# MoBA's probabilities turned by VectorE and a trip through DRAM, branch projections by halves of two chunks, x loaded later

## The chip, the cores and the metric

The kernel runs on one core of one Trainium2 chip. The metric is device microseconds of one execution. A core has a matrix engine (TensorE, "PE" in the profile, with its weight loads shown as "PEld"), a vector engine (VectorE, "DVE"), an activation engine (ScalarE, "ACT"), GpSimd ("POOL") and SyncE ("SP"), which here only issues DMAs. Each engine works through its own instructions strictly in the order in which the program was written for it, and waits at an instruction until what it needs is there.

## What is computed

Two decoder layers on 256 tokens of 1024 features, all in float32. Each layer is a gated mixer of two attentions, then a SwiGLU. Cut to what matters here:

```python
proj = x @ w_in                       # -> q, k, v of 8 stick-breaking heads, q, k, v of 8 MoBA heads, 2 gates
o_sb = stick_breaking_attention(...)
o_mb = moba_attention(...)            # 256 tokens are one block: causal softmax(q k^T / 8) v
branch_sb = merge_heads(o_sb) @ w_branch_sb
branch_mb = merge_heads(o_mb) @ w_branch_moba
merged = sigmoid(g_sb) * branch_sb + sigmoid(g_mb) * branch_mb
x = layer_norm(alpha * x + merged @ w_out)
x = layer_norm(alpha * x + (silu(x @ w_gate) * (x @ w_up)) @ w_down)
```

## The kernel before

**Numbers in two parts.** Every float32 operand of a product is split into a rounded part ("hi", a float32r copy made by ACT) and the rest ("lo", a subtraction by DVE); a product is three matmuls, hi·hi, hi·lo and lo·hi (`mm3`, line 424). Weights come as 122 granules per layer of 128x1024 numbers (512 KB). SP loads each into one of six `raw` buffers (line 135), ACT casts it into a ring slot `whi`, and DVE subtracts into `wlo` (lines 166 and 169). The rings hold ten granules; a slot is given free (`ws.allow`) when the matmuls of its old granule have been written. Seven granules per layer go another way, by DMAs that POOL issues (lines 182 and 200).

**One order, made when the kernel is built.** A planner, `Weave`, keeps an estimated time for PE, ACT and DVE. The main program writes PE's large matmuls; everything else is a generator (a "side") that yields the estimated time at which its next step is due, and `tick` runs the due ones after each three matmuls. Whatever a step emits takes its place at that moment in each engine's order. Nothing is reordered on the chip. `finish` runs sides to their end where the program needs their result.

**Attention.** Heads are handled in four pairs p = 0 to 3. For MoBA (`mb_line`, line 663) the scores of two pairs are made together (`two_pairs`), masked, their maximum taken (DVE), exponentiated with a running sum (ACT) and scaled by the reciprocal (DVE). The probabilities are 128 queries x 768 (two heads x three blocks of 128 keys), and have to be turned, so that keys lie on the partitions. `weighted` (line 564) does that with six PE transposes into a PSUM tile `pT` and then splits it into `pp` (ACT cast, DVE subtraction), of which there is one buffer. `both_parts` (line 605) multiplies by v (four matmuls, tiles `o`), and an ACT copy and DVE adds into `f` (one buffer) and a split give `o_mb`, hi and lo.

**Turning by another way.** `bounce_line` (line 502) was there already, for q and k of MoBA and a part of the SwiGLU: DVE transposes 32x32 blocks, SP stores the tile to DRAM and loads it back in four DMAs, which put the blocks in their places.

**Gates, branches, output.** Gate chunks c = 0 to 7 (tiles `pg`, 48 matmuls each) run while the attention of the pairs is worked off. Then `weave.finish(sides)` (line 875) waits for all attention, and the branch projections follow chunk by chunk (tiles `pb`, 24 matmuls of the stick-breaking half, 24 of the MoBA half, granule `G + 40 + c` with both halves), each merged by DVE into `m` and split. The output projection (tiles `pw`) then reads `m` chunk by chunk, first for the tokens 0 to 127.

## Time and profile before

| what | value |
|---|---|
| median of three runs | 726.14 us (726.01 to 726.39) |
| the profiled execution | 726.34 us |
| its span, first to last instruction | 724.5 us |
| around the span | 1.8 us |
| instructions | 12760 |
| mean granted TensorE clock | 0.997 |
| moved by DMA | 149.96 MB, mean 207 GB/s |

A page of the profile lists each engine's busy time and groups of instructions (line, engine, operation, output<-inputs, count, busy us, mean ns, idle time of the engine before them and what ended it). The chain of waits goes back from the last instruction to whatever released it each time, and so shows what set the end. The timeline lists single instructions with start and duration; "x4" merges four, and a bracket tells how long the engine had been idle and for whom.

### The profile page before, as it was taken

The numbers are of one execution on the slowest core, as the hardware profiler recorded it, in microseconds if no ns is written. First come the engines' busy times: TensorE is split into PE (matmuls) and PEld (weight loads), VectorE is DVE, ScalarE is ACT, GpSimd is POOL, SyncE is SP. The second block draws the span as 40 slices with busy tenths as digits, with TensorE's granted clock in tenths as the row PEclk, the third lists the DMA queues.
The fourth block names the chain that finished last, engine by engine and source line by source line (L and its number), as shares of the span: only waits on it lengthen the run. The fifth ranks groups of instructions, "written<-read, shape, count | busy, mean of one in ns | idle before, by whom it ended". The sixth has DMA issues, their size and how long they took to land.

```text
span 724.5 us, 12760 instructions
## 1 busy us (share of the span) xinstructions
PE 714.0 (99%) x5032; PEld 657.0 (91%) x5032; DVE 524.1 (72%) x792; ACT 391.0 (54%) x589; POOL 33.5 (5%) x48
## 2 busy tenths in 40 slices
PE   9999999999999999999999999999999999999995
PEld 7889899998899999988889889999888999998885
DVE  5999877796886666643688887877889776665416
ACT  5767687663665554442365566775556555454300
POOL 0001110000000000000000111100010000000001
PEclk9999999999999999999999999999999999999998
DMA  8899884575596656476259679745748865663501
GB/s 294 337 340 265 266 204 139 204 216 190 181 338 211 202 181 199 146 295 197 76 179 349 163 193 245 201 126 191 267 144 285 290 203 182 199 202 96 224 1 59
DMA packets 53532, 149.96 MB, mean 207 GB/s; under 512 B 10080, under 2 KB 17248, under 8 KB 53472
## 3 DMA queue, kind: packets, MB, share of 16 engines
q1 hardware_dynamic: 49296, 134.21, 55.2%
q0 software_dynamic: 4032, 14.68, 9.0%
q8 instruction: 39, 0.64, 0.4%
q10 hardware_dynamic: 144, 0.26, 0.1%
q14 instruction: 21, 0.17, 0.1%
HBM read 144.93 MB, written 4.19 MB: 206 GB/s over the span
## 4 chain that ended last, share of the span: by engine, by line
PE 96%; DVE 2%; DMA 0%; ACT 0%; issue 0%; POOL 0%; POOLq 0%; DVEq 0%
PE l1pf L418 14%; PE l0pf L418 14%; PE l0pd L418 8%; PE l0pg L418 6%; PE l1pg L418 6%; PE l1pe L418 4%; PE l1pd L418 4%; PE l1pqk L418 3%; PE l0pqk L418 3%; PE l0pw L418 3%; PE l1pvq L418 3%; PE l0pft L418 3%; PE l1pw L418 3%; PE l1pft L418 3%; PE l0pb L418 3%; PE l1pb L418 3%
## 5 line engine op out<-in xcount | busy, mean ns | idle before, releaser
L53 DVE TENSOR_TENSOR wlo<-raw,whi 128x1024 fp32r<-128x1024 f32 (+1 forms) x234 | 277.8, 1203 | 73.6 <-ACT whi L48 70.0
L48 ACT CAST whi<-raw 128x1024 fp32r<-128x1024 f32 (+1 forms) x233 | 237.9, 1036 | 82.2 <-PE l0pd L418 19.6
L418 PE MATMUL l1pf<-xT_hi,wlo 128*128 128x256 f32 x288 | 79.6, 276 | 0.0
L418 PE MATMUL l1pf<-xT_hi,whi 128*128 128x256 f32 x288 | 79.6, 276 | 0.0
L418 PE MATMUL l1pf<-xT_lo,whi 128*128 128x256 f32 x288 | 79.6, 276 | 0.0
L418 PE MATMUL l0pf<-xT_hi,wlo 128*128 128x256 f32 x288 | 79.5, 276 | 0.0
L418 PE MATMUL l0pf<-xT_hi,whi 128*128 128x256 f32 x288 | 79.5, 276 | 0.0
L418 PE MATMUL l0pf<-xT_lo,whi 128*128 128x256 f32 x288 | 79.5, 276 | 0.0
L418 PEld LDWEIGHTS l1pf<-xT_hi,whi 128*128 128x128 f32 x288 | 54.1, 188 | 0.0
L418 PEld LDWEIGHTS l1pf<-xT_lo,whi 128*128 128x128 f32 x288 | 54.1, 188 | 0.0
L418 PEld LDWEIGHTS l1pf<-xT_hi,wlo 128*128 128x128 f32 x288 | 54.1, 188 | 0.0
L418 PEld LDWEIGHTS l0pf<-xT_hi,whi 128*128 128x128 f32 x288 | 54.1, 188 | 0.0
L418 PEld LDWEIGHTS l0pf<-xT_lo,whi 128*128 128x128 f32 x288 | 54.1, 188 | 0.0
L418 PEld LDWEIGHTS l0pf<-xT_hi,wlo 128*128 128x128 f32 x288 | 54.1, 188 | 0.0
L418 PE MATMUL l0pg<-xT_hi,whi 128*128 128x256 f32 x128 | 36.2, 282 | 0.8 <-DVE l0vmb L53 0.8
L418 PE MATMUL l1pg<-xT_hi,whi 128*128 128x256 f32 x128 | 36.0, 282 | 0.0
L418 PE MATMUL l0pg<-xT_hi,wlo 128*128 128x256 f32 x128 | 35.5, 277 | 0.0
L418 PE MATMUL l1pg<-xT_hi,wlo 128*128 128x256 f32 x128 | 35.5, 277 | 0.0
L418 PE MATMUL l0pg<-xT_lo,whi 128*128 128x256 f32 x128 | 35.5, 277 | 0.0
L418 PE MATMUL l1pg<-xT_lo,whi 128*128 128x256 f32 x128 | 35.4, 277 | 0.0
L418 PE MATMUL l0pd<-whi,l0h_hi 128*128 128x512 f32 x88 | 34.5, 391 | 0.0
L418 PE MATMUL l0pd<-wlo,l0h_hi 128*128 128x512 f32 x88 | 34.3, 389 | 0.0
(347 smaller groups left out, 1790.6 us busy)
## 6 DMA issues: line engine op xcount, KB each, us to landing
raw<-in_w_dram SPq DMA_DIRECT2D x226, 512.0 KB, 4.4
whi<-in_w_dram POOLq DMA_DIRECT2D x14, 512.0 KB, 5.6
wlo<-in_w_dram POOLq DMA_DIRECT2D x14, 512.0 KB, 7.1
ln<-in_ln_dram SPq DMA_DIRECT2D x8, 512.0 KB, 5.4
raw<-in_w_dram SPq DMA_DIRECT2D x7, 256.0 KB, 5.8
x<-in_x_dram SPq DMA_DIRECT2D x2, 512.0 KB, 8.6
out_dram<-x SPq DMA_DIRECT2D x3, 256.0 KB, 2.0
xT_raw<-in_xT_dram SPq DMA_DIRECT2D x4, 128.0 KB, 4.1
```

The source lines that it names most:

```text
L48: f(*args, **kw)
L53: f(*args, **kw)
L418: nc.tensor.matmul(o, a, b, start=start, stop=stop)
```

## The change

It does five things.

1. MoBA's probabilities are no longer turned by PE. `mb_line` hands them to a new `bounced`, which calls `bounce_line` with six blocks (a DVE transpose of 128x768, a store of 384 KB and four loads of 96 KB per pair) and then splits what came back into `pp`. Stick-breaking keeps `weighted`.
2. The scores of pairs 2 and 3 wait for the exponentials of pairs 0 and 1 (`turned.append` moves into `mb_line`), no longer for their turned tiles; the fixed pause `MB_GAP` goes.
3. Branches are computed by halves: `branch(i, b, ...)` makes two chunks 2i and 2i+1 of one branch b. The stick-breaking branch (tiles `pa`) comes first, beside the last MoBA pairs; the MoBA branch (tiles `pb`) takes heads 0 to 3 first (k = 0, 1), then k = 2, and the last pair (k = 3) last. A granule holds two chunks of one branch, which `moved` loads in pieces of 2 KB per partition from two granules of the old layout.
4. The last pair's product with v goes into PSUM tiles of the `M` kind (`in_M`) and takes no turn for the `C` kind.
5. The two loads of x (512 KB each) are issued at 118 instead of 60 on the planner's clock.

```diff
         queue.dma_start(self.raw[g][:, sl], self.w[ORDER[g], :, sl])
         self.dma_t += 0.73

+    def moved(self, start, dst, g, **kw):
+
+        b, i = divmod(g % NG_LAYER - 40, 4)
+        if 0 <= b < 2:
+            g += i - 4 * b
+            start(dst.rearrange("p (c n) -> p c n", c=2),
+                  self.w[g:g + 2, :, b * 512:(b + 1) * 512].rearrange("c p n -> p c n"), **kw)
+        else:
+            start(dst, self.w[ORDER.get(g, g)], **kw)
+
     def load(self, upto):

         while self.loaded < min(upto, len(self.hard)):
             g = self.hard[self.loaded]
             before = self.hard[self.loaded - NRAW] if self.loaded >= NRAW else None
             self._open(g)
-            self.nc.sync.dma_start(self.raw[g], self.w[ORDER.get(g, g)])
+            self.moved(self.nc.sync.dma_start, self.raw[g], g)
             self.dma_t = max(self.dma_t, self.ready.get(before, 0.0) + 0.5) + 1.46
             self.there[g] = self.dma_t + 1.0
             self.loaded += 1
...
         nc.sync.dma_start(ident, ident_in)
         nc.sync.dma_start(rope, rope_in)
         nc.sync.dma_start(mask, mask_in)
-        yield 60.0
+        yield 118.0
         for t in range(2):
             nc.sync.dma_start(xs[t], x_in[t * P:(t + 1) * P, :])

...
         for h, hs in enumerate(ROWS):
             left[i] = dve(e, S, nc.vector.tensor_sub, oT[1][hs, p, :], o[hs, h, :], oT[0][hs, p, :].bitcast(F32))

-    def both_parts(name, p, v, oT, e):
+    def bounced(name, p, src, there, v, oT, e):
+
+        pT, e = yield from bounce_line(name, there, there, src, 6, e)
+        begun.append(name)
+        mine = len(begun)
+        while len(summed) < mine:
+            yield
+        e = max(e, summed[-1])
+        yield e
+        parts = (blocked(pp[:, i].rearrange("p h (k c) -> p (h k) c", c=P)) for i in range(2))
+        e = yield from split_line(*parts, pT, 768, e)
+        yield from both_parts(name, p, v, oT, e, p == NPAIR - 1)
+
+    def both_parts(name, p, v, oT, e, in_M=False):

         turns = []
-        for h in range(2):
-            turns.append((yield from turn(e)))
-        os = [bankC(f"{name}_o{h}", [P, 2, S]) for h in range(2)]
+        if in_M:
+            os = [bankM(f"{name}_o{h}", [P, 2, S]) for h in range(2)]
+        else:
+            for h in range(2):
+                turns.append((yield from turn(e)))
+            os = [bankC(f"{name}_o{h}", [P, 2, S]) for h in range(2)]
         pe_after(e)
         for h, o in enumerate(os):
             vs = [x[:, p, 2 * h:2 * h + 2, :].rearrange("p r c -> p (r c)") for x in v]
...
         yield e
         for h, o in enumerate(os):
             for i in range(2):
-                e = left[turns[h]] = dve(e, S, nc.vector.tensor_add, f[ROWS[h]], o[ROWS[h], i, :], f[ROWS[h]])
+                e = dve(e, S, nc.vector.tensor_add, f[ROWS[h]], o[ROWS[h], i, :], f[ROWS[h]])
+            if not in_M:
+                left[turns[h]] = e
         yield e
         yield from split_line(oT[0][:, p, :], oT[1][:, p, :], f, S, e)

...
             e = dve(e, 2 * (b - a), nc.vector.tensor_reduce, nmax[:, :, i], s[:, :, a:b],
                     axis=AX.X, op=OP.max, negate=True)
         yield e
-        ex = work.tile([P, 2, 384], F32, tag="T", name=f"{name}_e")
+        flat = work.tile([P, 768], F32, tag="T", name=f"{name}_e")
+        ex = flat.rearrange("p (h c) -> p h c", h=2)
         for h, i, a, b in BLOCKS:
             e = act(e, b - a + 200, nc.scalar.activation, ex[:, h, a:b], s[:, h, a:b], AF.Exp,
                     bias=nmax[:, h, i:i + 1], accum_out=ssum[:, h, i:i + 1])
         done.append(name)
+        turned.append(e)
         yield e
         rec = small.tile([P, 2, 2], F32, tag="rec", name=f"{name}_rec")
         dve(e, 32, nc.vector.reciprocal, rec, ssum)
         for h, i, a, b in BLOCKS:
             e = dve(e, b - a, nc.vector.tensor_scalar, ex[:, h, a:b], ex[:, h, a:b], rec[:, h, i:i + 1],
                     None, op0=OP.mult)
-        yield from weighted(name, p, ex, v, oT, e)
+        if p < 2:
+            there = (page0 if p else work).tile([P, 768], F32, tag="T", name=f"{name}_turn")
+        else:
+            there = unit(f"{name}_turn", [P, 1024])[:, :768]
+        yield from bounced(name, p, flat, there, v, oT, e)

     def two_pairs(line, name, ps, qks, free, e, sides, *args):

...
         def mb_two(p):
             while len(sigmoids) < NPAIR:
                 yield
-            yield weave.t + MB_GAP * p
             yield from two_pairs(mb_line, f"{L}mb", (p, p + 1),
                                  [[[part[:, i, :] for part in t] for t in (q_mb, k_mb)] for i in (p, p + 1)],
                                  l * 2 * NPAIR + NPAIR + p, 0.0, sides, v_mb, o_mb, exps)

         for p in (0, 2):
             sides.append(weave.add(mb_two(p)))
+        mb = len(sides)
         for c in range(1, KC):
             gate(c, G + 24 + 2 * c)
-        weave.finish(sides)
-        for dst in waiting:
-            act(0.0, 512, nc.scalar.activation, dst, dst, AF.Sigmoid)
+
+        def rooted():
+            for dst in waiting:
+                act(0.0, 512, nc.scalar.activation, dst, dst, AF.Sigmoid)
+            waiting.clear()
+
+        def branch(i, b, ps, ks=range(4)):
+            g = G + 40 + 4 * b + i
+            hi, lo = (x.rearrange("p (c k n) -> p c k n", c=2, k=4) for x in ws.take(g))
+            o = (o_sb, o_mb)[b]
+            for c in range(2):
+                for k in ks:
+                    mm3(ps[:, c, :], hi[:, c, k, :], lo[:, c, k, :], o[0][:, k, :], o[1][:, k, :],
+                        c == k == 0, c == 1 and k == 3)
+            if ks[-1] < 3:
+                return 0.0
+            ws.allow(g + NSPLIT)
+            gated = gates[i][:, :, b, :]
+            return dve(pe_done(), 512, nc.vector.tensor_mul, gated, gated, ps)
+
+        if len(exps) == NPAIR:
+            rooted()
+        for i in range(4):
+            if i % 2 == 0:
+                ps = bankB(f"{L}pa{i}", [P, 2, 2, S])
+            branch(i, 0, ps[:, i % 2])
+        weave.finish(sides[:mb])
+        weave.finish(sides[:-2])
+        rooted()


         gb = load_gb(l, 0)
         m_t = [pair_tiles(f"{L}m{i}", [P, 4, S]) for i in range(2)]

-        def m_parts(c):
-            return m_t[c // 4][0][:, c % 4, :], m_t[c // 4][1][:, c % 4, :]
-
-        banks = {}
-        for c, b in ((0, 0), (1, 0), (0, 1), (1, 1), *((c, b) for c in range(2, KC) for b in range(2))):
-            g = G + 40 + c
-            hi, lo = ws.take(g)
-            hi = hi.rearrange("p (b k n) -> p b k n", b=2, k=4)
-            lo = lo.rearrange("p (b k n) -> p b k n", b=2, k=4)
-            if b == 0:
-                banks[c] = bankM(f"{L}pb{c}", [P, 2, S])
-            ps, o = banks[c], (o_sb, o_mb)[b]
-            for k in range(4):
-                mm3(ps[:, b, :], hi[:, b, k, :], lo[:, b, k, :],
-                    o[0][:, k, :], o[1][:, k, :], k == 0, k == 3)
-            if b == 0:
-                continue
-            ws.allow(g + NSPLIT)
-            mt = work.tile([P, 2, S], F32, tag="T", name=f"{L}mt{c}")
-            dve(pe_done(), 512, nc.vector.tensor_mul, mt, gates[c // 2][:, c % 2], ps)
-            e = dve(0.0, S, nc.vector.tensor_add, mt[:, 0, :], mt[:, 0, :], mt[:, 1, :])
-            weave.add(split_line(*m_parts(c), mt[:, 0, :], S, e), e)
+        def m_parts(c, n=1):
+            return [m[:, c % 4:c % 4 + n, :] if n > 1 else m[:, c % 4, :] for m in m_t[c // 4]]
+
+        pbs = [x for i in range(2) for x in bankB(f"{L}pb{i}", [P, 2, 2, S]).rearrange("p i c n -> i p c n")]
+        for ks, upto in ((range(2), -1), (range(2, 3), None)):
+            for i in range(3):
+                branch(i, 1, pbs[i], ks)
+            weave.finish(sides[:upto])
+        for i in range(4):
+            e = branch(i, 1, pbs[i], range(3 if i < 3 else 0, 4))
+            a, b = (gates[i][:, :, j, :] for j in range(2))
+            e = dve(e, 512, nc.vector.tensor_add, a, a, b)
+            weave.add(split_line(*m_parts(2 * i, 2), a, 512, e), e)


         norms = []
```

Where the instructions stand now, in three places of layer 0 (layer 1 has the same pattern in all three).

PE, the product of the last pair (`l0mb3_o`) with v. Before, 42 matmuls into a gate chunk (`l0pg6`) stood between pair 2's product and pair 3's, and these rows are how pair 2's product ended and the 42 began:

```order
L418 MATMUL l0mb2_o1_1543<-pp_168,l0vmb0_800 128x512
L418 MATMUL l0mb2_o1_1543<-pp_168,l0vmb1_801 128x2x128
L418 MATMUL l0pg6_1484<-xT_hi_108,whi_98 128x256
L418 MATMUL l0pg6_1484<-xT_lo_109,whi_98 128x256
L418 MATMUL l0pg6_1484<-xT_hi_108,wlo_99 128x256
```

Now 18 matmuls of the stick-breaking branch (`l0pa2`) stand between the two products. These are the last three of them, the last pair's product, and the first of the MoBA branch (`l0pb0`):

```order
L427 MATMUL l0pa2_1679<-l0osb_hi_328,whi_98 128x256
L427 MATMUL l0pa2_1679<-l0osb_lo_329,whi_98 128x256
L427 MATMUL l0pa2_1679<-l0osb_hi_328,wlo_99 128x256
L427 MATMUL l0mb3_o0_1751<-pp_168,l0vmb0_798 128x512
L427 MATMUL l0mb3_o0_1751<-pp_168,l0vmb1_799 128x2x128
L427 MATMUL l0mb3_o1_1752<-pp_168,l0vmb0_798 128x512
L427 MATMUL l0mb3_o1_1752<-pp_168,l0vmb1_799 128x2x128
L427 MATMUL l0pb0_1766<-l0omb_hi_1020,whi_98 128x256
```

So the last pair's product moved nearer to that of the pair before it, and the MoBA branch stands right behind it.

DVE, from the adds of pair 2 to the first merge (`raw47` to `raw50` are the weight granules that the subtraction into `wlo` belongs to). Before:

```order
L53 TENSOR_TENSOR l0mb2_f_1555<-l0mb2_o0_1542,l0mb2_f_1555 64x256 x2
L53 TENSOR_TENSOR l0mb2_f_1555<-l0mb2_o1_1543,l0mb2_f_1555 64x256 x2
L53 TENSOR_TENSOR pp_168<-l0mb3_pT_1522,pp_168 128x768
L53 TENSOR_TENSOR l0omb_lo_1023<-l0mb2_f_1555,l0omb_hi_1022 128x256
L53 TENSOR_TENSOR wlo_99<-raw44_1267,whi_98 128x1024
L53 TENSOR_TENSOR l0mb3_f_1620<-l0mb3_o0_1608,l0mb3_f_1620 64x256 x2
L53 TENSOR_TENSOR l0mb3_f_1620<-l0mb3_o1_1609,l0mb3_f_1620 64x256 x2
L53 TENSOR_TENSOR wlo_99<-raw45_1283,whi_98 128x1024
L53 TENSOR_TENSOR l0omb_lo_1023<-l0mb3_f_1620,l0omb_hi_1022 128x256
L53 TENSOR_TENSOR l0mt0_1707<-l0gate0_937,l0pb0_1668 128x512
```

Now, ahead of the first merge:

```order
L53 TENSOR_TENSOR l0mb2_f_1727<-l0mb2_o0_1718,l0mb2_f_1727 64x256 x2
L53 TENSOR_TENSOR l0mb2_f_1727<-l0mb2_o1_1719,l0mb2_f_1727 64x256 x2
L53 TENSOR_TENSOR pp_168<-l0mb3_turn_1415,pp_168 128x768
L53 TENSOR_TENSOR l0gate3_1455<-l0gate3_1455,l0pa2_1679 128x2x256
L53 TENSOR_TENSOR wlo_99<-raw47_1491,whi_98 128x1024
L53 TENSOR_TENSOR l0omb_lo_1021<-l0mb2_f_1727,l0omb_hi_1020 128x256
L53 TENSOR_TENSOR l0mb3_f_1777<-l0mb3_o0_1751,l0mb3_f_1777 64x256 x2
L53 TENSOR_TENSOR l0mb3_f_1777<-l0mb3_o1_1752,l0mb3_f_1777 64x256 x2
L53 TENSOR_TENSOR wlo_99<-raw48_1504,whi_98 128x1024
L53 TENSOR_TENSOR wlo_99<-raw49_1537,whi_98 128x1024
L53 TENSOR_TENSOR l0omb_lo_1021<-l0mb3_f_1777,l0omb_hi_1020 128x256
L53 TENSOR_TENSOR wlo_99<-raw50_1556,whi_98 128x1024
```

A gate product and two more weight subtractions have come in between. The merges of all eight chunks follow now in one piece, where they stood chunk by chunk between the weight subtractions before:

```order
L53 TENSOR_TENSOR l0gate0_935<-l0gate0_935,l0pb0_1766 128x2x256
L53 TENSOR_TENSOR l0gate0_935<-l0gate0_935 128x2x256
L53 TENSOR_TENSOR l0gate1_1131<-l0gate1_1131,l0pb0_1766 128x2x256
L53 TENSOR_TENSOR l0gate1_1131<-l0gate1_1131 128x2x256
L53 TENSOR_TENSOR l0gate2_1306<-l0gate2_1306,l0pb1_1767 128x2x256
L53 TENSOR_TENSOR l0gate2_1306<-l0gate2_1306 128x2x256
L53 TENSOR_TENSOR l0m0_lo_1763<-l0gate0_935,l0m0_hi_1762 128x512
L53 TENSOR_TENSOR l0gate3_1455<-l0gate3_1455,l0pb1_1767 128x2x256
L53 TENSOR_TENSOR l0gate3_1455<-l0gate3_1455 128x2x256
L53 TENSOR_TENSOR wlo_99<-raw51_1666,whi_98 128x1024
L53 TENSOR_TENSOR l0m0_lo_1763<-l0gate1_1131,l0m0_hi_1762 128x512
```

SP, the trips of pairs 2 and 3 among the weight loads (`scr` is the tile in DRAM), where before only weight loads stood:

```order
L134 DMA raw45_1442<-in_w_dram 128x2x512
L518 DMA l0mb2_scr_1379<-l0mb2_turn_1378 128x768
L134 DMA raw46_1477<-in_w_dram 128x2x512
L518 DMA l0mb3_scr_1416<-l0mb3_turn_1415 128x768
L134 DMA raw47_1491<-in_w_dram 128x2x512
L137 DMA raw48_1504<-in_w_dram 128x1024
L523 DMA l0mb2_turn_1378<-l0mb2_scr_1379 32x4x192 x4
L137 DMA raw49_1537<-in_w_dram 128x1024
L137 DMA raw50_1556<-in_w_dram 128x1024
L523 DMA l0mb3_turn_1415<-l0mb3_scr_1416 32x4x192 x4
L421 DMA x0_106<-in_x_dram 128x1024
```

Ten new DMAs and the first load of x stand among the weight loads, and each is issued only when the one ahead of it has been.

More of the change, by code (lines that the diff above doesn't have):

```diff
@@ L181, in cast_line @@
             self.parts[g] = [self._part(i, g) for i in range(2)]
-            e = weave.pool(weave.t, nc.gpsimd.dma_start, self.parts[g][0], self.w[ORDER.get(g, g)])
+            e = weave.pool(weave.t, self.moved, nc.gpsimd.dma_start, self.parts[g][0], g)
             self.dma_t = max(self.dma_t, e + 1.0) + 2.2
@@ L199, in rest_line @@
                 yield e
-            e = weave.pool(e, nc.gpsimd.dma_start, lo, self.w[ORDER.get(g, g)], accum_op=OP.add)
+            e = weave.pool(e, self.moved, nc.gpsimd.dma_start, lo, g, accum_op=OP.add)
             self.dma_t = max(self.dma_t, e + 1.0) + 2.2
@@ L251 @@
 MARGIN = 0.29
-MB_GAP = 8.85
 T0 = 4.1
```

## The prediction

> **What bounds the kernel.** I read the page's busy times and chain first, then its groups, then the chain and the timelines of the stretch that changes.
>
> ```profile
> span 724.5 us, 12760 instructions
> PE 714.0 (99%) x5032; PEld 657.0 (91%) x5032; DVE 524.1 (72%) x792; ACT 391.0 (54%) x589; POOL 33.5 (5%) x48
> PE 96%; DVE 2%; DMA 0%; ACT 0%; issue 0%; POOL 0%; POOLq 0%; DVEq 0%
> L418 PE MATMUL l0pg<-xT_hi,whi 128*128 128x256 f32 x128 | 36.2, 282 | 0.8 <-DVE l0vmb L53 0.8
> 72.00:135.00 63.00, 62.20 (x523) 59.62 (x522) 50.54 (x94) 43.93 (x89) 6.02 (x9) 1.00 0.71 203
> ```
>
> PE is at work in 714.0 of 724.5 us and makes 96% of the chain. So whatever leaves PE's queue shortens the run, and whatever makes PE wait lengthens it. The fourth row holds the one wait of PE in mid-kernel, 0.8 us. The last is the MoBA stretch of layer 0 (us, then PE, PEld, DVE, ACT and POOL busy, clock, DMA share, GB/s): PE at 62.2 of 63 us and full clock, DVE with 12.5 us to spare.
>
> **What leaves PE.** The chain through that stretch (start, us, what):
>
> ```profile
> 101.89 0.66 PE l0mb_pT L431 x6
> 102.55 1.06 PE l0pg L418 x9
> 103.61 0.66 PE l0mb_pT L431 x6
> ...
> 111.18 1.57 PE l0mb_s L550 x24
> 112.75 0.89 PE l0mb_o L418 x4
> ...
> 125.93 0.70 PE l0mb_o L418 x4
> 126.62 4.82 PE l0pg L418 x42
> 131.44 0.70 PE l0mb_o L418 x4
> 132.14 2.77 PE l0pg L418 x24
> 134.91 21.76 PE l0pb L418 x192
> 156.67 3.47 PE l0pw L418 x15
> ```
>
> The six transposes of a pair take 0.66 us, and there are eight pairs in two layers: 8 x 0.66 = 5.3. Around them matmuls start a little late: single rows at 101.61 and 102.50 enclose a pair's six and one more matmul,
>
> ```profile
> 101.61 0.28 PE L418 MATMUL l0pg<-xT_hi,wlo 128*128 128x256 f32 x1
> 101.73 0.82 PE L431 MATMUL l0mb_pT<-ident,l0mb_e 128*128 128x128 f32 x6
> 102.30 0.37 PE L418 MATMUL l0pg<-xT_hi,whi 128*128 128x256 f32 x1
> 102.50 0.28 PE L418 MATMUL l0pg<-xT_lo,whi 128*128 128x256 f32 x1
> ```
>
> 0.89 us where two matmuls would take 2 x 21.76/192 = 0.23, thus 0.66 to 0.70 a pair with the last start. A product with v right behind scores costs 0.89, not 0.70; that place is gone, some 0.1 per layer net of another switch. **Gain: 5.6 us** (5.3 to 5.9). The matmuls of the branches are the same 384, only in another order.
>
> **The wait at 79 us stays.** Loading x later takes 1 MB out of the DMA queues there, and ACT waited for k's trip just then (last row). But DVE was the one PE waited for:
>
> ```profile
> 77.39 0.96 DVE L53 TENSOR_TENSOR l0sb_beta<-l0sb_beta,l0sb_inc 128x766 f32<-128x766 f32 x1
> 78.27 0.68 DVE L53 TENSOR_TENSOR l0kmb_lo<-l0kmb_tok,l0kmb_hi 128x512 fp32r<-128x512 f32 x1
> 78.87 0.68 DVE L53 TENSOR_TENSOR l0vmb<-l0pu,l0vmb 128x512 fp32r<-128x512 f32 x1
> 78.69 0.62 ACT L48 CAST l0kmb_hi<-l0kmb_tok 128x512 fp32r<-128x512 f32 x1 [2.57 <-DMA l0kmb_tok<-l0kmb_scr]
> ```
>
> DVE goes back to back through its three rows, and none of them needs that cast; so v's subtraction, for which PE waits, could not have started sooner, and the order there is unchanged. I take 0, with -0.8 as the other end. In its new place x is covered: it is read only after the output projection, over 20 us later.
>
> **First new wait: the last pair.** `bounced` emits the subtraction into `pp` and, for the last pair, the product with v in the same step. PE has 18 matmuls (2.0 us) since pair 2's product; before it had 42 (4.82). What lies between those two products on ACT and DVE I read from pair 2 to 3 before:
>
> ```profile
> 126.31 0.76 ACT L48 COPY l0mb_f<-l0mb_o 64x256 f32<-64x256 f32 x2 [0.43 <-PE l0mb_o L418]
> 127.09 0.80 ACT L48 CAST pp<-l0mb_pT 128x768 fp32r<-128x768 f32 x1
> ...
> 127.24 1.78 DVE L53 TENSOR_TENSOR l0mb_f<-l0mb_o,l0mb_f 64x256 f32<-64x256 f32 x4
> 129.05 0.96 DVE L53 TENSOR_TENSOR pp<-l0mb_pT,pp 128x768 fp32r<-128x768 f32 x1
> ```
>
> From pair 2's product (start 125.93) to `pp` ready (130.01) are 4.1 us. Now a weight subtraction ends at about the same place ahead of the adds, and I reckon 4.0. PE arrives after 0.70 + 18 x 0.1133 = 2.74. **PE waits 1.25 us per layer, 2.5 in all.** Ends: were the adds late by another weight subtraction, 1.2 more each; were they to start with ACT's first copy, 0.4 less. Everything behind on PE waits with it.
>
> **Second new wait: the output projection.** From there DVE has a list without a gap. Its spacing, start to start, I read where rows followed one another:
>
> ```profile
> 139.10 0.69 DVE L53 TENSOR_TENSOR l0mt<-l0gate,l0pb 128x512 f32<-128x512 f32 x1 [2.80 <-PE l0pb L418]
> 139.82 0.42 DVE L53 TENSOR_TENSOR l0mt<-l0mt 128x256 f32<-128x256 f32 x1
> 140.16 1.22 DVE L53 TENSOR_TENSOR wlo<-raw,whi 128x1024 fp32r<-128x1024 f32 x1
> 141.30 0.68 DVE L53 TENSOR_TENSOR l0mt<-l0gate,l0pb 128x512 f32<-128x512 f32 x1
> ```
>
> A weight subtraction takes 1.14, 512 columns 0.60 (78.27 to 78.87 above), 0.71 if the next row needs the result, 256 columns 0.34. After `pp`: gate product 0.60, weights 1.14, `omb_lo` of pair 2 0.42, ACT's copy, which waits for it since `f` has one buffer, 0.45, four adds 1.74, two weights 2.28, `omb_lo` of pair 3 0.34, weights 1.14, three merges 3 x 1.31, and `m_lo` of the first two chunks 0.68: 12.7 us, less 0.08 overlap at the start. PE in that time: 0.70 for the product, 96 x 0.1133 = 10.88 for the MoBA branch, then 0.45 until the third matmul of `pw` (2 x 3.47/15), the first that reads `m_lo`: 12.05. **PE waits 0.6 per layer.** In layer 0 the next `m_lo` stands behind another weight subtraction, 0.3 more; in layer 1 it is ahead of it. On the way `omb_lo` of pair 3 is ready 7.0 us after `pp` by the same list, and PE asks for it after 0.70 + 55 x 0.1133 = 6.9: nothing worth a term. **1.5 us in all**, ends 0 (DVE 0.7 faster per layer) and 3.0 (whole durations in place of the spacings, 0.7 more per layer).
>
> **What is hidden.** DVE's transposes of 768 columns have no row; those of 256 and 512 have,
>
> ```profile
> L53 DVE STREAM_TRANSPOSE l0hb<-l0sg 128x256 f32<-128x256 f32 x4 | 1.8, 446 | 0.1
> L53 DVE STREAM_TRANSPOSE l0kmb_tok<-l0kmb_tok 128x512 f32<-128x512 f32 x2 | 1.4, 711 | 0.1
> l0kmb_scr<-l0kmb_tok SPq DMA_DIRECT2D x2, 256.0 KB, 3.5
> l0kmb_tok<-l0kmb_scr SPq DMA_DIRECT2D x8, 64.0 KB, 6.9
> l1kmb_scr<-l1kmb_tok SPq DMA_DIRECT2D x2, 256.0 KB, 7.0
> raw<-in_w_dram SPq DMA_DIRECT2D x226, 512.0 KB, 4.4
> 92.11 9.78 PE l0pg L418 x84
> 99.77 0.24 ACT L48 ACTIVATION_READ_ACCUMULATOR l0mb_e<-l0mb_s,l0mb_nmax 128x1 f32 x1
> ```
>
> and 0.265 more for each 256 gives 0.98, an estimate: 3.9 us per layer within the 12.5 that DVE has free; without that cover they would add to the chain above at 0.98 each. A trip through DRAM has a store (3.5 to 7.0 us to landing) and loads (4.4 to 6.9). In layer 0 the scores of pairs 2 and 3 now follow 75 matmuls after the first scores, at 92.11 + 75 x 0.1164 = 100.8 (the row at 92.11: 9.78/84) instead of 111.18; the exponentials whose PSUM they take are done at 100.0, 0.8 ahead. SP holds pair 2's store behind weight loads that wait for DVE to free a `raw` buffer: one subtraction waits, through ACT, for gate chunk 5, 138 matmuls behind the scores, near 118; so I put the store at 116, the loads, behind two more weight loads, at 124 to 125, landed by 132. Pair 2's product comes 201 + 42 + 69 matmuls and two products behind the scores, 102.4 + 312 x 0.1145 + 1.4 = 139.5, and ACT and DVE need 2.5 us ahead of it for the split: 5 us to spare. Pair 3's loads land some 3 us later and its product is due 4 us later. Behind the waiting DMAs stand weight loads for granules used more than 10 us later, so those can wait. The branch weights in 2 KB pieces I cost at nothing for the same reason: even twice 4.4 us lies inside that lead.
>
> **Sum.** Against the profiled execution, 726.34: -5.6 + 2.5 + 1.5 = -1.6. That execution lies 0.2 above the median of the three, 726.14, so I forecast **724.5**, 0.2% less, about what a measurement of this kernel can tell from no change.
>
> **Rivals.**
>
> *The merges hide* (second wait 0, the first near 0.8): for it speaks that DVE had slack in this stretch; against, that its list has no gap between `pp` and `m_lo`. -5.6 + 1.6 = -4.0: 722.1.
>
> *DVE's list is longer than its spacing says* (whole durations, or one weight subtraction more ahead of the adds): waits of 5.5 instead of 4.0, 726.0, no change to be seen.
>
> *The turned pairs come late,* the way to slower. ACT's cast of a turned pair stands ahead of weight casts, so a late load stops both. From a landing 5 us later than reckoned each further us is one on PE, in each layer; from 6.5 us the run is slower than before by what can be told. If store and loads took half as long again at their longest (7.0 + 6.9, thus 7 more), they would be late by 2 per layer: -1.6 + 4 = +2.4, 728.5. For it speaks that issues sit behind weight loads; against it that loads with the same pattern landed in 6.9 in their slowest group. The Trainium skill has a rule against this way of turning: VectorE: DVE Perf Modes, "The three transpose paths" and "Rules for kernel authors", would turn 128x128 on TensorE and warns that a plain DMA with strides is 19 times slower than the one with a transpose unit, 1309 ns for 128x128 in its table; by that I estimate 25 us for each of a pair's six blocks, which nothing here would hide. The rows of k's trip do not agree: its four loads together moved 256 KB within 6.9 us each, since DVE has turned the 32x32 blocks and the DMA moves whole runs.
>
> *The change doesn't do what it says on the path* (transposes gone, but PE waits for the same DVE work anyway, 5.6 given back): 726.1.
>
> **Chances.** Forecast 48% (723.7 to 725.4, half of it beyond 0.2% faster), merges hide 26%, longer list 13%, late 8%, given back 5%. Faster by over 0.2% (below 724.7): 0.26 + 0.27 = 0.53. Slower by over 0.2%: 0.08. Within: 0.39. Range 721.5 to 726.8: it covers the forecast, the merges' case and most of the longer list and of the given back, and leaves out the late turn and a case without any wait (720.5).
>
> **What would show it.** No transposes of MoBA on PE, 48 fewer instructions. A wait of PE of about 1.25 us for DVE's `pp` ahead of the last pair's product, in both layers, and one of 0.3 to 0.9 for `m_lo` at the start of `pw`; 0.8 still at 79 us; no wait for the turned tiles. I am wrong if PE waits for ACT's `pp` cast or for `whi` (late trips), or if it doesn't wait at all.

## The result, and the profile after

| | before | changed kernel |
|---|---|---|
| median, four runs each | 726.12 us (726.01 to 726.39) | 734.78 us (734.4 to 735.09) |
| ratio to before, 95% interval | | 1.0116 (1.0104 to 1.0129) |
| profiled execution, and its span | 726.34 and 724.5 us | 734.4 and 732.5 us |
| last matmul ends, in the span | 716.42 us | 724.85 us |

The change makes the kernel 8.7 us slower. The forecast was 1.6 us faster, and the range ended at 726.8.

The page of the changed kernel, its span, busy times and shares of the chain:

```profile
span 732.5 us, 12710 instructions
PE 712.8 (97%) x4984; PEld 652.8 (89%) x4984; DVE 529.2 (72%) x784; ACT 389.1 (53%) x579; POOL 34.5 (5%) x48
PE 92%; DVE 4%; DMA 2%; issue 1%; ACT 0%; POOL 0%; DVEq 0%; POOLq 0%; SPq 0%; ACTq 0%
```

The 48 transposes are gone (4984 matmuls for 5032), and PE is busy for 1.2 us less. But the span is 8.0 us longer, and DVE's share of the chain has doubled: PE now waits. For what, the view of waits says (engine and line that waited, for whom; us in total, times, longest):

```profile
PE l0pb L427 <- DVE l0gate L53: 2.4, 2, 1.4
PE l1pb L427 <- DVE l1gate L53: 2.4, 2, 1.4
PE l0pa L427 <- DVE l0gate L53: 1.6, 2, 0.9
PE l1pa L427 <- DVE l1gate L53: 1.6, 2, 0.8
...
PE l1mb_o L427 <- DVE pp L53: 0.8, 1, 0.8
PE l0mb_o L427 <- DVE pp L53: 0.8, 1, 0.8
```

The waits for `pp` were forecast. The four rows above them were not: in each layer PE stops twice in `pa` and twice in `pb` until DVE has multiplied a gate by a branch's product (`l0gate<-l0gate,l0pa`). The timeline of PE shows the stop, here all four in layer 0:

```profile
132.99 0.28 PE L427 MATMUL l0pa<-l0osb_hi,wlo 128*128 128x256 f32 x1
134.12 0.38 PE L427 MATMUL l0pa<-l0osb_hi,whi 128*128 128x256 f32 x1 [0.85 <-DVE l0gate L53]
134.34 0.28 PE L427 MATMUL l0pa<-l0osb_lo,whi 128*128 128x256 f32 x1
...
139.62 0.28 PE L427 MATMUL l0pa<-l0osb_hi,wlo 128*128 128x256 f32 x1
140.67 0.39 PE L427 MATMUL l0pa<-l0osb_hi,whi 128*128 128x256 f32 x1 [0.78 <-DVE l0gate L53]
...
153.03 0.28 PE L427 MATMUL l0pb<-l0omb_hi,wlo 128*128 128x256 f32 x1
154.30 0.39 PE L427 MATMUL l0pb<-l0omb_hi,whi 128*128 128x256 f32 x1 [0.99 <-DVE l0gate L53]
...
155.66 0.28 PE L427 MATMUL l0pb<-l0omb_hi,wlo 128*128 128x256 f32 x1
157.36 0.39 PE L427 MATMUL l0pb<-l0omb_hi,whi 128*128 128x256 f32 x1 [1.43 <-DVE l0gate L53]
```

Matmuls of this size otherwise start every 0.114 us. So the bracket says too little: from start to start PE loses 1.13 - 0.11, and the first matmul behind a stop takes 0.22 (134.12 to 134.34), 0.11 more than the others. That makes 1.12, 1.05, 1.27 and 1.70 us, 5.1 per layer, **10.3 in all**. DVE's side of the first stop:

```profile
133.37 0.69 DVE L53 TENSOR_TENSOR l0gate<-l0gate,l0pa 128x512 f32<-128x512 f32 x1 [3.92 <-ACT l0mb_f L48]
```

DVE was idle, began as soon as the 24 matmuls of branch half 0 were through (the last ends at 133.27; the copy that the bracket names ends at the same moment, 133.29), took 0.69, and only then did PE begin half 1. Nothing of half 1 needs that result. What ties the two together is the place where they lie: `ps = bankB(f"{L}pa{i}", [P, 2, 2, S])` is made for i = 0 and 2 only, one tile of 4 KB per partition, and halves 0 and 1 are its two parts of 2 KB; so are 2 and 3, and in `pb` likewise. In the program's order, printed with what each instruction waits for, the first matmul of half 1 carries a wait of its own:

```
L427 MATMUL l0pa0_1609<-l0osb_hi_328,wlo_99 128x256
L427 MATMUL l0pa0_1609<-l0osb_hi_328,whi_98 128x256 [waits DVE_49]
```

So the program lets the second part of a tile be written only after the last reader of its first part. Before, every chunk had a 2 KB tile (`bankM`) to itself, and was read once, when both of its halves were done.

### The profile page after: what moved, and what is told of

The parts are those of the page before. It is cut to its first block, busy times and chain, and to the rows that moved or that the text cites. A ratio compares the mean times of both kernels' runs of the same rounds, so it can differ in the third digit from the quotient of the medians.

```text
span 732.5 us, 12710 instructions
## 1 busy us (share of the span) xinstructions
PE 712.8 (97%) x4984; PEld 652.8 (89%) x4984; DVE 529.2 (72%) x784; ACT 389.1 (53%) x579; POOL 34.5 (5%) x48
## 4 chain that ended last, share of the span: by engine, by line
PE 92%; DVE 4%; DMA 2%; issue 1%; ACT 0%; POOL 0%; DVEq 0%; POOLq 0%; SPq 0%; ACTq 0%
PE l1pf L427 13%; PE l0pf L427 13%; PE l0pd L427 8%; PE l0pg L427 6%; PE l1pg L427 6%; PE l1pe L427 4%; PE l1pd L427 4%; PE l1pft L427 3%; PE l0pw L427 3%; PE l1pqk L427 3%; PE l0pft L427 3%; PE l1pvq L427 3%; PE l1pw L427 3%; PE l0pqk L427 2%; PE l0pv L427 2%; PE l1pk L427 2%
## 5 line engine op out<-in xcount | busy, mean ns | idle before, releaser
L427 PE MATMUL l0pd<-whi,l0h_lo 128*128 128x512 f32 x88 | 34.3, 389 | 0.0
```

Of the source, the lines that this page charges most:

```text
L427: nc.tensor.matmul(o, a, b, start=start, stop=stop)
```

## Experiments

**Theory A:** the tiles shared by two branch halves make PE wait, 10.3 us. **Theory B:** VectorE's list is too long in this stretch, and PE waits for it wherever that shows first. **Theory C:** the turned pairs, or the branch weights in 2 KB pieces, come late. In the table, each time stands beside that of the kernel before on the same chip.

| run | this | before | ratio, 95% |
|---|---|---|---|
| x1_pa_tiles | 731.12 | 726.46 | 1.0058 (1.0039 to 1.0078) |
| x2_own_tiles | 726.57 | 726.46 | 0.9996 (0.9984 to 1.0007) |
| b1_before_shared | 735.36 | 726.46 | 1.0109 (1.0084 to 1.0134) |
| z1_bounce_alone | 742.16 | 726.46 | 1.0200 (1.0165 to 1.0236) |
| w1_merge_order | 725.32 | 726.30 | 0.9989 (0.9980 to 0.9998) |
| y3_late_product | 727.32 | 726.30 | 1.0008 (0.9999 to 1.0018) |
| x3_x_early | 726.49 | 726.30 | 0.9999 (0.9990 to 1.0009) |
| d1_double_turn | 735.34 | 726.30 | 1.0125 (1.0110 to 1.0140) |
| w2_pw_bank | 725.48 | 726.37 | 0.9989 (0.9980 to 0.9998) |
| w5_product_later | 727.36 | 726.37 | 1.0014 (1.0005 to 1.0023) |
| w4_weights_held | 731.53 | 726.37 | 1.0066 (1.0054 to 1.0079) |
| w7_pool_adds | 731.64 | 726.46 | 1.0073 (1.0059 to 1.0087) |
| z6_half_turned | 727.94 | 726.60 | 1.0013 (1.0003 to 1.0022) |

### Tiles: x1, x2, b1

x1 only pairs the halves of `pa` in another way, so that neighbours in time lie in different tiles:

```diff
+        pas = []
         for i in range(4):
-            if i % 2 == 0:
-                ps = bankB(f"{L}pa{i}", [P, 2, 2, S])
-            branch(i, 0, ps[:, i % 2])
+            if i < 2:
+                pas.append(bankB(f"{L}pa{i}", [P, 2, 2, S]))
+            branch(i, 0, pas[i % 2][:, i // 2])
```

> The changed kernel, with one thing altered: the MoSA-side branch products (pa) alternate between the two 4 KB PSUM tiles (branches 0 and 2 in one, 1 and 3 in the other; before 0 and 1, 2 and 3). Theory A (a PSUM tile shared by two branches makes the second branch's first matmul wait until VectorE has read the first branch out): the two waits of PE inside pa, 1.12 and 1.05 us from start to start with the slow matmul behind each, go from both layers: 2 x 2.17 = 4.3 less, 730.4; the waits ahead of the last pair's product and inside pb stay. Theory B (VectorE's list is too long there and PE waits for it wherever it stands): the same time is waited ahead of pair 2's or pair 3's product, and the time stays within 1 us of 734.8. Theory C (turned pairs, or branch weights in 2 KB pieces, come late): PE waits sooner for pair 2, again 734 to 735.

x2 also gives each half of `pb` a tile of its own:

```diff
-        pbs = [x for i in range(2) for x in bankB(f"{L}pb{i}", [P, 2, 2, S]).rearrange("p i c n -> i p c n")]
+        pbs = [bankC(f"{L}pb{i}", [P, 2, S]) for i in range(2)]
+        pbs += [bankB(f"{L}pb{i}", [P, 2, 2, S])[:, 0] for i in range(2, 4)]
```

> As the run with pa's tiles altered, and the four MoBA-side products (pb) in a PSUM tile of their own each (two 2 KB tiles that the pairs' products leave, two halves of the 4 KB tiles). Theory A: the two waits inside pb, 1.27 and 1.70 us with the slow matmul behind each, go as well: 2 x (2.17 + 2.97) = 10.3 less than the changed kernel, 724.5; if the first halves of the output projection then wait for m_lo (0.6 per layer by the prediction), 725.7. Theory B: little of it is won, over 730. The wait of about 1 us per layer ahead of the last pair's product stays under both.

b1 does the reverse to the kernel before: two chunks in one tile.

```diff
             if b == 0:
-                banks[c] = bankM(f"{L}pb{c}", [P, 2, S])
+                if c % 2 == 0:
+                    two = bankB(f"{L}pb{c}", [P, 2, 2, S])
+                banks[c] = two[:, c % 2]
```

> The kernel before, with one thing altered: the eight chunks of the branch projections lie two by two in the 4 KB PSUM tiles, not each in a tile of 2 KB of its own. Nothing is turned through DRAM here and nothing is read or written twice in one bank. Theory A: four times per layer (chunks 1, 3, 5, 7) PE waits for VectorE to have read the chunk before out of the other half: 1.1 us each, where VectorE is free, 8 x 1.1 = 8.8 more, 734.9. Theories B and C: no such wait, 726.1.

(The "MoSA side" of the first of these texts is the stick-breaking branch.) x1 wins 3.7 of 4.3 us and x2 8.2 of 10.3 (4.0 and 8.55, if each run is taken against the kernel before on its own chip). In both, as in b1, every engine has the same instructions in the same order as the kernel that was edited; only the tiles differ. b1, which has nothing of the change but the sharing, is 8.9 slower, and its waits are where theory A puts them, four per layer:

```profile
PE l0pb L418 <- DVE l0mt L53: 3.6, 4, 0.9
PE l1pb L418 <- DVE l1mt L53: 3.5, 4, 0.9
```

This is shown from both sides: the sharing makes the slowdown. What x2 falls short of the 10.3 is told by its own waits, of which x1 has the first two as well:

```profile
PE l0mb_o L427 <- DVE pp L53: 1.2, 1, 1.2
PE l1mb_o L427 <- DVE pp L53: 1.2, 1, 1.2
...
PE l0pw L427 <- DVE l0m_lo L53: 0.4, 1, 0.4
```

In layer 0 pair 2's product begins 2.2 us sooner than in the changed kernel (139.29 for 141.47), but the last pair's `pp` is ready only 1.75 sooner (143.44 for 145.19). From start to start, with the slow matmul behind it, the wait for `pp` thus grows from 1.15 to 1.57 us per layer, and the wait of the output projection for `m_lo`, which was hidden behind the other stops, comes out: 0.78 in layer 0 (0.58, and 0.20 at the next `m_lo`) and 0.58 in layer 1. Those are 2.2 us given back; 10.3 - 2.2 = 8.1, and 8.2 was measured.

### The turning alone: z1, d1, z6

z1 takes the bounce into the kernel before, and with it the earlier scores of pairs 2 and 3; projections, weights and x stay as they were.

```diff
-        yield from weighted(name, p, ex, v, oT, e)
+        yield from bounced(name, p, flat, there, v, oT, e)
...
-            yield weave.t + MB_GAP * p
```

> The kernel before, with the turning of MoBA's probabilities through DRAM alone (scores of pairs 2 and 3 early, as in the change); branch projections in the old order with all four pairs done ahead of them, weights in 4 KB pieces, x loaded at the old time. Theory A: the transposes leave PE (5.6 less) and nothing is waited for on account of shared tiles: 720.5 to 722.5. Theory C (the trips through DRAM come late, or the extra transposes of VectorE put it behind): PE waits ahead of the products of pairs 2 or 3, which now stand some 10 us earlier relative to the projections' end: 726 or more.

16 us slower by the medians (its four executions lie between 739.8 and 743.8): here theory C holds. The chain through layer 0 (start, us, what), in the longest of the four:

```profile
127.87 6.68 DMA l0mb_turn<-l0mb_scr
134.56 0.02 issue
...
135.52 0.97 DVE pp L53
136.49 0.14 issue
136.62 0.99 PE l0mb_o L427 x2
...
140.53 0.97 DVE pp L53
141.50 0.14 issue
141.64 1.62 PE l0mb_o L427 x4
```

PE had come to pair 2's product at 131. Its data landed at 134.6, and pair 3 then stands behind one more round of product, copy, adds and `pp`. In the changed kernel pair 2's tile landed at 131.1 and pair 3's at 135.5, and that is early enough, since most of the stick-breaking branch (78 of 96 matmuls) lies ahead of pair 2's product, which begins at 141.5: there is no wait for a turned tile in its list of waits, nor one for `whi`. So theory C is out for the change as it stands. That the new order of the branches is what hides the trips is read from the two traces; no run took that order alone.

d1 gives the transposes of the kernel before twice, into the same place:

```diff
-                transpose(pT[:, h, cs], wt[:, h, cs])
+                for _ in range(2 if len(v[0].shape) == 4 else 1):
+                    transpose(pT[:, h, cs], wt[:, h, cs])
```

> The kernel before, with each of MoBA's 48 transposes on TensorE given twice into the same place. It measures the gain alone: the prediction's price (0.66 to 0.70 us for the six of a pair, eight pairs) makes it 5.3 to 5.6 slower, 731.4 to 731.8. Were part of a transpose hidden beside other work of PE, less; were there something behind them that waits, more.

9.0 slower, not 5.5, and the reason lies in the edit: the condition holds for the stick-breaking pairs too, so 96 transposes came twice. The chain shows a pair's twelve (start, us, what):

```profile
103.60 1.31 PE l0mb_pT L431 x12
```

Six more take 0.655; 16 x 0.655 = 10.5, and the wait at 79 us, 0.96 from start to start, is gone here because PE comes later. That leaves 9.5 for 9.0 measured. The price per pair is confirmed; that one gets it back by taking them away is not.

z6 therefore turns only pairs 0 and 1 through DRAM, in the old order of the projections, and takes the MoBA-side terms in the order of pairs 2, 3, 0, 1.

```diff
+        if p < 2:
+            yield from bounced(name, p, flat, there, v, oT, e)
+        else:
+            yield from weighted(name, p, ex, v, oT, e)
```

> The kernel before, with only pairs 0 and 1 turned through DRAM, whose trips have the time (their exponentials are done some 10 us ahead of those of pairs 2 and 3); pairs 2 and 3 are turned on TensorE as before; branch projections in the old order with the tiles of their own, the MoBA-side terms taken in the order of pairs 2, 3, 0, 1. If the gain of the prediction is real as a gain (0.66 us for the six transposes of a pair, with nothing that waits in their place), four groups less make 2.6: 723.5, and up to 1 us per layer back where the last pair's product stands right ahead of the projections: 723.5 to 725.5. Rival (on this kernel VectorE, not TensorE, sets the end of this stretch, so what leaves TensorE comes back as a wait): 726 or more.

Its list of waits for PE:

```profile
PE l1mb_o L427 <- DVE pp L53: 2.0, 1, 2.0
...
PE l0mb_o L427 <- DVE pp L53: 1.3, 1, 1.3
```

From start to start these are 2.1 and 1.5 us, together more than the 2.6 saved, and behind the longer one the granted clock fell to half for 3.41 us in the profiled execution (last section). The eleven executions lie between 726.48 and 728.7, none below the kernel before by more than that kernel's own scatter. In layer 0 the four products now stand between 118.8 and 134.4 us, where before they stood between 105.5 and 131.3, and between two products stands a chain of ACT and DVE (copy, four adds, cast, `pp`) that PE cannot shorten. So on this kernel turning less on PE was no gain even without shared tiles.

### What is left: w1, w2, y3, w5, w4, w7, x3

x2 is level with the kernel before, though PE has 5.6 us less to do. The view by stretches (us, then PE, PEld, DVE, ACT and POOL busy, clock, DMA share, GB/s) says why; first the kernel before, then x2:

```profile
137.00:157.00 20.00, 20.00 (x177) 19.92 (x176) 17.66 (x29) 12.10 (x19) 0.00 (x0) 1.00 0.70 230
```

```profile
137.00:157.00 20.00, 18.34 (x148) 17.37 (x147) 19.05 (x30) 10.88 (x18) 0.00 (x0) 1.00 0.75 247
```

DVE is busy for 19.05 of 20 us. And x2's chain of waits holds no work of PE from 139.84, ACT's copy behind pair 2's product, to 156.53, the first matmul that reads `m_lo`; three of its pieces:

```profile
139.84 0.37 ACT l0mb_f L48
142.48 0.96 DVE pp L53
155.87 0.61 DVE l0m_lo L53
```

So DVE, with ACT's share of the chain, and not PE, sets the pace here. w1 splits each merged pair of chunks as soon as the next one's sum is given:

```diff
-            weave.add(split_line(*m_parts(2 * i, 2), a, 512, e), e)
+            merges.append(weave.add(split_line(*m_parts(2 * i, 2), a, 512, e), e))
+            weave.finish(merges[:i])
```

> The run with own tiles, and the merges taken apart: the split of branch i's sum (m_lo) is put on VectorE's list right behind the sum of branch i+1, no longer behind all three. Theory A (what is left over the kernel before is the two waits of the prediction, for pp and for m_lo): m_lo of the first two chunks is ready 1.3 us sooner, so the wait at the start of the output projection, 0.58 to 0.78 us per layer there, goes: 1.4 less than the run with own tiles, 725.2. Rival (PE is held there by the weights or by something else in the list): 726.6.

725.32, as expected, and with w2 the fastest of all: 0.1% below the kernel before (0.9980 to 0.9998), too little to build on. y3 adds a `yield e + MARGIN` ahead of the last pair's product, which holds it back until its operand is due on the planner's clock, lets all four halves of `pb` do their first three quarters ahead of the last (`range(4)` and `range(3, 4)` in the loops), and has each merge's split finished ahead of the matmuls of `pw` that read it:

> The run with the merges taken apart, and the last pair's product given when its operand is due by the planner: it comes 24 branch matmuls (2.7 us) later in PE's order, and all four MoBA-side products do their first three quarters ahead of the last ones. Theory A: the wait for pp (1.41 us and 0.16 of slow matmuls per layer in the run with own tiles) goes, 3.1 less; VectorE's list from pp to the first m_lo is the next to be waited for, up to 1 us per layer back: 721.5 to 724. Rival (a wait moved is a wait kept: the same VectorE list ends at the same time whatever PE's order): 725 or more.

```profile
PE l0pw L427 <- DVE l0gate L53: 2.1, 1, 2.1
```

The wait for `pp` is gone, and one of 2.1 stands at the output projection in its place, in layer 1 as well: the rival. The row names a gate product, and there is a reason in the tiles again: `pw` takes the 4 KB tile that half 2 of `pb` leaves. w2 therefore swaps the tiles of w1 (halves 0 and 1 in `bankB`, 2 and 3 in `bankC`):

> The run with the merges taken apart, with the four MoBA-side products in their own tiles the other way round: the first two in the 4 KB tiles, the last two in the 2 KB tiles, so that the output projection's first 4 KB tile is the one that the first branch leaves, not the third. Theory A (the same rule: a tile makes its next writer wait for its last reader): the wait at the start of the output projection, 0.39 us per layer for the third branch's gate product, goes: 0.8 less than 725.3, 724.5. Rival (m_lo or the weights hold it there too): 725.3.

725.48, no gain: the wait for the gate product goes, and PE waits later in `pw` for weights (`wlo`) instead, from start to start 0.3 us in layer 0 and 0.6 in layer 1. The remaining three have the late product with it: w5 alone, w4 with the weight subtractions held back, w7 with the tiles mixed and the sums on GpSimd (`nc.gpsimd.tensor_tensor` in place of `nc.vector.tensor_add`).

> The run with the other order of tiles, and the last pair's product 24 branch matmuls (2.7 us) later in PE's order, three branches ahead of the last quarter as in the change. Theory A: the wait of 1.4 us and 0.16 of slow matmuls per layer for pp goes (3.1 in all); VectorE's list from pp to the last pair's omb_lo, three weight subtractions among it, ends near 150 and PE asks for it near 148.6, so up to 1.4 per layer comes back there: 721.5 to 724. Rival (as in the run with the late product, a wait moved is a wait kept): 724.5 or more.

> As the run with the later product, and the weight subtractions for granules three or more ahead are held back on VectorE's list from the last pair's pp until the second merge is given. Theory A (VectorE's list in that stretch is what PE waits for, and nothing else): omb_lo and the first m_lo come 1 to 2.3 us sooner, no wait is left between pp and the output projection: 726.1 - 5.6 and 0.5 for waits that are as before = 720.5 to 721.5. Rival (weights held back are late afterwards, or their raw buffers stop SP's loads): waits for whi or wlo in the output projection, 723 or more.

> The run with the later product, with the first MoBA-side product in the first 4 KB tile, the second and third in the 2 KB tiles and the fourth in the second 4 KB tile (the wait of 0.77 us per layer for the last pa gate product goes: 1.5 less than 727.4), and the four sums of two gated products per layer on GpSimd, not VectorE. Theory A (from the last pair's pp to the output projection's weights, VectorE's list is what PE waits for): three sums of 0.65 less ahead of the weight subtractions take away the 1.5 us per layer that the output projection waits for its weights: 722.5 to 724.5. Rival (GpSimd takes over 1.5 us for a sum of 128x512, and m_hi and m_lo come later by it): 725.5 or more.

All three fall to their rivals, w7 though its rival's condition (over 1.5 us for a sum on GpSimd) was not met. The longest waits of PE, one fence for each of w5, w4, w7, and the group of the sums on GpSimd:

```profile
PE l0pw L427 <- DVE wlo L53: 1.3, 1, 1.3
```

```profile
PE l0pw L431 <- DVE wlo L53: 2.7, 1, 2.7
```

```profile
PE l0pw L427 <- DVE wlo L53: 2.2, 1, 2.2
L58 POOL TENSOR_TENSOR l0gate<-l0gate 128x512 f32<-128x512 f32 x4 | 5.5, 1380 | 39.9 <-DMA raw<-in_w_dram 38.6 <-DVE l0gate L53 1.2
```

In every one of them PE ends up waiting for the weights of the output projection, whose subtractions stand on DVE behind the merges; held back in w4, they come later still. w5 and w4 also wait 0.8 us per layer at half 1 of `pb`, whose 4 KB tile the last gate product of `pa` still reads; w7, which has other tiles, waits 1.0 us per layer in `pb` for ACT's `omb_hi`. A sum takes 1.38 us on GpSimd and 0.69 on DVE, and the weight subtractions stand behind splits that wait for it. Theory B thus accounts for what remains after theory A: the edits to PE's order mostly chose which item of DVE's list was waited for. That a shorter list would win the 5.6 us is not shown, since w7, meant to shorten it, put a slower sum into the same chain.

x3 sets x2's x loads back to 60.

> The run with own tiles, and x loaded at the old time (60 on the planner's clock, not 118). The prediction costs this edit at nothing: within 0.5 of the run with own tiles, 726.6. Rival (the 1 MB in the queues matters, for the wait at 79 us or for the loads of the turned pairs): over 1 us away from it, to either side.

726.49 beside 726.57: loading x later costs and brings nothing.

## Why the prediction was wrong, point by point

**The step that failed** is a sentence of the part on what leaves PE: "The matmuls of the branches are the same 384, only in another order." Their number is right, and I looked for new waits at two places only, at `pp` and at `m_lo`. I did not ask where the sums of the halves lie and who reads the neighbouring part. That step was costed at nothing and measured 10.3 us in the changed kernel's timeline; x2 took 8.2 of it away again, and b1, by sharing alone, made the old kernel 8.9 slower. It was not among the rivals either; the only way to slower that I priced was a late trip. Nor could the signs of being wrong catch it: none of them came, and the wait for `pp` did. No run was needed to see it: the tile is in the diff, and the program's order names the wait at the instruction.

**The rest of the sum**, against rows and start-to-start distances of the profiled executions:

| term | forecast | measured |
|---|---|---|
| transposes and the late starts around them | -5.6 | -5.6 (4.6 in `pT`, 1.0 in `pg`) |
| wait for the last pair's `pp` | +2.5 | +2.3; in x2 +3.1 |
| wait of `pw` for `m_lo` | +1.5 | 0, hidden behind the stops; in x2 +1.4 |
| wait at 79 us | 0 | 0.8 still there; x3 tells no difference |
| turned pairs | hidden | no wait; z1 shows what they cost uncovered |
| weights in 2 KB pieces | hidden | weight loads to landing 4.7 us (4.4 before), no wait |
| stops at shared tiles | not seen | +10.3 |
| small waits (`omb` of pair 2, `pw`, `pft`) | 0 | about +1.4 |

The measured terms add to -5.6 + 2.3 + 10.3 + 1.4 = +8.4, and the ends of the last matmuls differ by 724.85 - 716.42 = 8.43; the medians differ by 8.7.

**What held.** The gain, both forecast waits (in x2, where nothing hides them, 1.57 per layer for 1.25 and 0.78 and 0.58 for 0.9 and 0.6), the landing of pair 2's tile in layer 0 (131.1 for 132), and the price of the transposes on DVE. That the changed kernel's own wait for `pp` (1.15) is near the forecast too is in part luck: `pp` was ready 3.7 us after pair 2's product began, not 4.0, since the stops had let DVE catch up, and a slow first matmul of 0.16 that the forecast leaves out made up for it; in x2 it was ready after 4.15. The rows for the transposes and trips:

```profile
L53 DVE STREAM_TRANSPOSE l0mb_turn<-l0mb_e 128x768 f32<-128x768 f32 x4 | 3.9, 979 | 0.1
l0mb_scr<-l0mb_turn SPq DMA_DIRECT2D x4, 384.0 KB, 4.9
l0mb_turn<-l0mb_scr SPq DMA_DIRECT2D x16, 96.0 KB, 5.3
l1mb_scr<-l1mb_turn SPq DMA_DIRECT2D x4, 384.0 KB, 8.0
```

0.979 us for 128x768 where I estimated 0.98 from the smaller rows, stores of 4.9 and 8.0 us (3.5 to 7.0 taken as bounds) and loads of 5.3. The rule of the Trainium skill against turning by DMA (VectorE: DVE Perf Modes, "The three transpose paths"), by which I estimated 25 us for each of a pair's six blocks, is about a copy that turns by its strides. It does not hold for a DMA that moves blocks which DVE has turned: these rows answer it. z1 shows that its advice can be right for another reason: where nothing covers the trip, PE waited up to 5.4 us at a pair. Two slips of mine changed nothing: 6.9 us for k's loads is a median, and single ones took up to 8.4 in layer 0; and half of 48% is 0.24, not the 0.27 in the chances.

**What was right but too small a thought:** "From there DVE has a list without a gap." I used it for one wait. x2's chain shows that it holds for the whole stretch, and the runs from w1 to w7 agree: with the tiles put right, 5.6 us less on PE came out as 1 us at the most (w1), and the forecast of -1.6 would have met +0.1 (x2).

**Open:** whether the halves need those waits on the chip, had the program not asked for them, was not tried; x2 removes the sharing, not the wait alone. And w1's 0.1% is too little to call it a better kernel.

## What to carry to other kernels

When work is reordered, list for each accumulator where it lies, who reads it, and what is written beside it in the same tile: here a tile was released whole, and a round trip PE to VectorE and back cost 1.05 to 1.70 us each time, eight times over. Then look at the program's order with its waits, not only at the order of names. And before taking work off the busiest engine, check in that very stretch how much the next engine has free; here it was 12% (17.66 of 20 us busy), and in x2 5% (19.05).

## What was not expected of the hardware

**A long wait costs more than its length.** The timeline of PE in w4, where it waited 3.1 us from start to start, and the view by stretches right behind it:

```profile
155.83 0.40 PE L431 MATMUL l0pw<-whi,l0m_hi 128*128 128x512 f32 x1
158.95 0.79 PE L431 MATMUL l0pw<-wlo,l0m_hi 128*128 128x512 f32 x1 [2.72 <-DVE wlo L53]
159.54 0.63 PE L431 MATMUL l0pw<-whi,l0m_lo 128*128 128x512 f32 x1
159.96 0.63 PE L431 MATMUL l0pw<-whi,l0m_hi 128*128 128x512 f32 x1
160.39 0.63 PE L431 MATMUL l0pw<-wlo,l0m_hi 128*128 128x512 f32 x1
```

```profile
159.00:162.50 3.50, 3.50 (x9) 2.78 (x10) 3.50 (x4) 2.30 (x4) 0.00 (x0) 0.54 0.70 192
```

Behind the wait matmuls start every 0.43 us, not 0.23, for some 3 us. The granted clock of the whole stretch is 0.54; from 158.81 to 162.22, for 3.41 us, it is 0.50, and 1.00 on both sides. z1 shows the same 0.50 behind its four waits, 5.7, 3.8, 5.5 and 3.1 us: 18.1 us together, yet its profiled span is 17.5 longer though 5.6 left PE, which leaves some 5 us, an estimate, to the slow clock and what comes with it.

How long a wait has to be for this, its length does not say. Those of 1.7 us (the changed kernel), 2.02, 2.34 and 2.35 us (y3) and one of 2.60 us (w7, layer 0) left the clock at 1.00; one of 2.25 us (z6, layer 1), one of 2.37 us (w2, at 79 us) and one of 2.61 us (w7, layer 1) did not. What parts them is where they lie. In all the traces here the granted clock is 1.00 or 0.50, and between two changes of it lie whole multiples of 3.41 us (w4: 153.60, 3.41, 354.99, 3.41, 204.80). So I cut each trace into windows of 3.41 us, counted from its first change; w7's two waits in these windows:

```profile
155.73:159.14 3.41, 2.67 (x12) 1.85 (x10) 2.18 (x4) 2.09 (x4) 2.91 (x2) 1.00 0.00 0
159.14:162.55 3.41, 1.95 (x9) 1.61 (x10) 3.41 (x4) 3.41 (x6) 0.00 (x0) 1.00 0.23 70
514.13:517.54 3.41, 1.19 (x6) 0.67 (x4) 2.87 (x4) 2.79 (x4) 1.10 (x1) 1.00 0.00 0
517.54:520.95 3.41, 3.41 (x10) 2.63 (x9) 3.41 (x4) 3.41 (x5) 0.00 (x0) 0.50 0.69 198
```

The wait of layer 0 lies across two windows, and PE is busy for 2.67 and 1.95 us in them; that of layer 1 lies in one, PE is busy for 1.19, and the next window runs at half clock. Over the fifteen traces, each window at full clock in which PE was idle for 1.84 us or less was followed by full clock, each in which it was idle for 1.97 us or more by half clock, and none lies between. (PE's busy time is as the profile models it.)

The Trainium skill (TensorE: Matmul & The Clock Gate, Part 1) tells of a clock that falls to half after an idle window of about 3.4 us and comes back after a busy one, with windows that run freely. The half, the window and its free run agree with these rows; but the window did not have to be idle throughout, 1.97 us of it were enough.

**The wait at 79 us is not the same in all executions:** its row in the list of waits reads 0.8 in most kernels, 1.6 in y3 and 2.0 in w2, though w1 (0.8) and w2 have the same instructions in the same order on every engine, and differ in later tiles alone. w2's profiled execution, 727.56 us, lies 2.1 above the median of its ten; a wait 1.2 longer and a stretch of half clock behind it are of that size.
